# Sevens in a form with plus signs in the weights' sums: two of the four sums by accumulating transfers on GpSimd's queue, two in place

## The chip, the cores and the metric

The kernel runs on one core of a Trainium2 chip. Its metric is the device time of one execution in microseconds. Before the change three runs took 2607.01, 2607.35 and 2611.01 us, so the median is 2607.35 us.

## What is computed

A decoder trunk of two layers on 256 tokens of width 2048, all in float32. Each layer is a token mixer and a SwiGLU feed-forward block, each with a norm ahead of it, a scale and shift from the conditioning vector, and a gate behind it. Layer 0 mixes by retention, layer 1 by a short gated convolution. The change lies in the feed-forward block of layer 1:

```python
def swiglu(h, w_in, w_out):
    a, b = jnp.split(h @ w_in, 2, axis=-1)
    return (jax.nn.silu(a) * b) @ w_out
...
        x = (x + g2 * swiglu(h, ffn_w_in[i], ffn_w_out[i])).astype(x.dtype)
```

Here `h` is 256 x 2048, `w_in` 2048 x 11264 and `w_out` 5632 x 2048.

## The kernel before

All weights are laid out by the host in the order of use, in chunks of 128 partitions x 2048 columns (1 MB). `fetch` (L381) takes one of three buffers named `raw` and has SyncE's queue (SP) load the next chunk into it. TensorE works on float32 as a sum of two rounded parts, so every chunk is split: `prepare` (L387) takes it in pieces; ScalarE rounds a piece to `hi` (L413) and VectorE subtracts that from the piece to get `lo` (L416). There are four buffers each of `hi` and `lo`, so a piece can be rounded as soon as TensorE has finished the piece four places ahead of it. The matmuls take `hi` and `lo` through `take` (L430). TensorE's order is the order of the program; the other engines' order is made by a scheduler that follows priorities, and each engine and queue then works strictly in its own order.

In the feed-forward block of layer 1 the tokens are the output's rows: `token_products` (L1193) computes a block of 256 tokens x 1024 columns, from steps of two 128-row tiles of the weights and two column blocks of 512. A step is one chunk of 1 MB, and there are two kinds:

- A plain step takes the chunk in two pieces of 1024 columns. Each of the four 128 x 512 blocks is multiplied with both halves of the tokens, three matmuls of 512 columns for each product (`triple`, L1182, L1187 to L1189): 24 matmuls.
- A step called seven computes the same 2 x 2 x 2 product of blocks with seven products in place of eight: 21 matmuls. It needs four sums of the activations' blocks (`seven_sums`, L630, made once and used by all column blocks), and four sums of the weights' blocks. Some of the seven products are collected in banks of their own (m1, m5, m6, m7) over all sevens of the block, and added to the output's blocks at the end (L1236 to L1241).

Write B11, B21 for the two row tiles in the first column block, and B12, B22 for those in the second. Before, a seven's chunk holds B11, B12, B22, B21 in that order, and the weights' sums are T1 = B12 - B11, T3 = B22 - B12, T2 = B22 - T1 and T4 = B21 - T2. VectorE makes them in a buffer of its own named `sums` (128 x 4 x 512, one buffer): T1 and T3 in one subtraction 1024 wide (L419), T2 (L423) and T4 (L425) in one each of 512. The seven's pieces are B11 alone (512 wide, one product), B22 and B21, T1 and T3, T2 and T4 (1024 wide, two products each). Since the last two pieces come out of `sums`, the chunk's `raw` buffer is free as soon as T4 is made.

There are 42 sevens: three in each of the ten column blocks of the first matrix that are done this way (30), and four in each of three blocks of the second matrix (12). Between two sevens stand one to three plain steps. The first eight chunks of the block are done in another form (`normed`, L664), which also takes the norm's root on the way: VectorE's L585, GpSimd's power on 128 x 2 numbers (L587) and TensorE's spreading of it (L594).

GpSimd's queue has in this part of the program nothing but that power, and it issues no transfer in the whole kernel.

Of the kernel before, what the change touches and what calls it, by code (L numbers as in the profile page):

```python
# [10 lines left out]
F32 = mybir.dt.float32  # L11
# [3 lines left out]
ALU = mybir.AluOpType  # L15
PSUM = bass.MemoryType.PSUM

P = 128
# [7 lines left out]
DV = 512  # L26
# [5 lines left out]
CHUNK = 2048  # L32
# [22 lines left out]
RAW_BUFS = 3  # L55
PART_BUFS = 4
# [8 lines left out]
class Group:  # L65
# [202 lines left out]
def trunk(ctx: ExitStack, tc: tile.TileContext, x_in, c_in, pos_in, w_mod, cols_in, tab_in, w_all, out):  # L268
    nc = tc.nc
# [8 lines left out]
    def name(s):  # L278
        serial[0] += 1
        return f"{s}_{serial[0]}"  # L280
# [87 lines left out]
    pieces, at_col = [], 0  # L368
    for _, _, g in in_use_order():
        width = sum(w for _, _, w in g.blocks())  # L370
        for o in range(-at_col % HALF, width, HALF):
            i = (at_col + o) % CHUNK
            if not g.seven:
                pieces.append(("plain", i))
            elif i == 0:
                pieces += [("seven", n) for n in range(4)]
        at_col += width
# [3 lines left out]
    def fetch():  # L381
        raw = wpool.tile([P, CHUNK], F32, tag="raw", name=name("raw"), bufs=RAW_BUFS)
        nc.sync.dma_start(raw, w_all[n_fetched[0]])
        n_fetched[0] += 1
        fetched.append(raw)

    def prepare(between=None):  # L387
# [10 lines left out]
        full = raws[0]  # L398
        if kind == "plain":
            raw = full[:, i : i + HALF]  # L400
        else:
            if i == 0:
                blocks[:] = [spool[0].tile([P, 4, DV], F32, tag="sums", name=name("sums"), bufs=1)]
            block = [full[:, n * DV : (n + 1) * DV] for n in range(4)]
            t1, t3, t2, t4 = [blocks[0][:, n, :] for n in range(4)]
# [12 lines left out]
        if kind == "seven" and i == 0:  # L418
            nc.vector.tensor_tensor(  # L419
                blocks[0][:, 0:2, :].rearrange("p a b -> p (a b)"), full[:, DV : 3 * DV], full[:, : 2 * DV],  # L420
                op=ALU.subtract,
            )
            nc.vector.tensor_tensor(t2, block[2], t1, op=ALU.subtract)  # L423
        elif kind == "seven" and i == 1:
            nc.vector.tensor_tensor(t4, block[3], t2, op=ALU.subtract)  # L425

    blocks, spool = [], []
# [203 lines left out]
    def seven_sums(full, tag):  # L631
# [4 lines left out]
        nc.vector.tensor_tensor(s1, a21, a22, op=ALU.add)  # L636
        nc.vector.tensor_tensor(s2, s1, a11, op=ALU.subtract)
        nc.vector.tensor_tensor(s3, a11, a21, op=ALU.subtract)
        nc.vector.tensor_tensor(s4, a12, s2, op=ALU.subtract)
# [554 lines left out]
    def token_products(steps, act, sums_of, then):  # L1194
# [8 lines left out]
        for n, g in enumerate(steps):  # L1203
            first, last = n == 0, n == len(steps) - 1
            if not g.seven:
# [15 lines left out]
                ("m1", a11), (x_banks[1][0], s4), (x_banks[0][0], a12), ("m5", s1), ("m7", s3), ("m6", s2),  # L1221
                (x_banks[0][1], a22),
# [11 lines left out]
            if g is sevens[-1]:  # L1234
                m1, m5, m6, m7 = [flat(m_banks[i]) for i in ("m1", "m5", "m6", "m7")]
                y11, y12, y21, y22 = values = [value(f"y{i}") for i in range(4)]  # L1236
                nc.scalar.copy(y11, m1)
                nc.vector.tensor_tensor(y12, m6, y11, op=ALU.add)
                nc.vector.tensor_tensor(y21, m7, y12, op=ALU.add)
                nc.vector.tensor_tensor(y12, m5, y12, op=ALU.add)  # L1240
                nc.vector.tensor_tensor(y22, m5, y21, op=ALU.add)  # L1241
# [185 lines left out]
```

## Time and profile before

| | |
|---|---|
| median of three runs | 2607.35 us (2607.01 to 2611.01) |
| the profiled execution's own time | 2605.66 us |
| its span in the profile | 2603.9 us |
| TensorE matmul, busy | 2571.1 us, 14341 matmuls |
| VectorE, busy | 2178.4 us |
| ScalarE, busy | 1300.3 us |
| GpSimd, busy | 129.6 us |
| mean rate of the transfers | 264 GB/s |

Times in the profile are counted from the start of the span. PE is TensorE (PEld its weight loads), DVE VectorE, ACT ScalarE, POOL GpSimd, SP SyncE's queue. A group's row gives the line in the kernel, the engine, the operation, what it writes and reads with its shape, how often it occurs, its busy time and mean time, and the idle time of its engine right before it with what ended it. The sevens lie between 1925 and 2513 us of the span.

### The profile page before, as it was taken

What the parts mean: (1) busy time and instruction counts of PE and PEld (TensorE: products, weight loads), DVE (VectorE), ACT (ScalarE), POOL (GpSimd) and SP (SyncE); (2) the same over time, 40 slices, a digit from 0 to 9 for tenths busy, and PEclk for the clock granted to TensorE, in tenths of its full rate; (3) what the DMA queues carried; (4) which work ended last, traced back from release to release, by engine and by line L of the source; (5) the groups of instructions that cost most, each with busy time, mean ns of one, the idle gap of its engine ahead of it and who ended that gap; (6) DMA issues with size and microseconds to landing.
All of it is one profiled execution on the core that took longest, in us unless ns stands there. A gap on an engine that the chain in (4) does not pass through costs nothing.

```text
span 2603.9 us, 36702 instructions
## 1 busy us (share of the span) xinstructions
PE 2571.1 (99%) x14341; PEld 2239.5 (86%) x14341; DVE 2178.4 (84%) x2751; ACT 1300.3 (50%) x1757; POOL 129.6 (5%) x230
## 2 busy tenths in 40 slices
PE   7999999999999999999999999999999999999998
PEld 5998889888889888888888898888898888888887
DVE  7998878787698887777777889888889999999984
ACT  5544543444456444334444454444565554555553
POOL 0000000120000010010000100000000000000000
PEclk9999999999999999999999999999999999999999
DMA  9976668777676887888887868877755555555553
GB/s 399 402 278 239 231 229 323 273 284 279 252 286 243 330 324 292 290 307 304 293 296 285 306 236 317 316 296 279 287 179 209 180 208 201 189 202 198 196 195 129
DMA packets 96945, 687.48 MB, mean 264 GB/s; under 512 B 10753, under 2 KB 12545, under 8 KB 13825
## 3 DMA queue, kind: packets, MB, share of 16 engines
q1 hardware_dynamic: 96194, 684.48, 71.2%
q8 instruction: 112, 1.84, 0.3%
q10 hardware_dynamic: 576, 0.66, 0.1%
q14 instruction: 63, 0.52, 0.1%
HBM read 682.99 MB, written 2.10 MB: 263 GB/s over the span
## 4 chain that ended last, share of the span: by engine, by line
PE 66%; issue 28%; DVE 3%; DMA 2%; ACT 1%; POOL 0%; SPq 0%; POOLq 0%; ACTq 0%; DVEq 0%
PE bank L475 29%; PE bank L478 15%; PE bank L514 4%; PE bank L513 4%; PE bank L515 4%; DMA raw<-w_all 2%; PE bank L499 1%; PE bank L498 1%; PE bank L500 1%; PE bank L688 1%; DVE lo L416 1%; PE bank L689 1%; PE bank L543 1%; PE bank L690 1%; PE bank L542 1%
## 5 line engine op out<-in xcount | busy, mean ns | idle before, releaser
L413 ACT CAST hi<-raw 128x1024 fp32r<-128x1024 f32 (+1 forms) x912 | 932.3, 1031 | 904.2 <-DMA raw<-w_all 268.3
L416 DVE TENSOR_TENSOR lo<-raw,hi 128x1024 fp32r<-128x1024 f32 (+1 forms) x912 | 1081.0, 1196 | 281.2 <-ACT hi L413 278.8
L475 PE MATMUL bank<-h,hi 128*128 128x512 f32 x2016 | 699.8, 391 | 0.0
L478 PE MATMUL bank<-h,lo 128*128 128x256 f32 x2016 | 564.4, 280 | 0.0
L475 PEld LDWEIGHTS bank<-h,hi 128*128 128x128 f32 x2016 | 377.0, 187 | 82.5
L327 DVE SCALAR_TENSOR_TENSOR raw<-raw,cb 128x2048 f32<-128x2048 f32 x160 | 365.8, 2286 | 33.0 <-DMA raw<-w_mod 32.6
L478 PEld LDWEIGHTS bank<-h,lo 128*128 128x128 f32 x2016 | 381.0, 189 | 0.0
L475 PE MATMUL bank<-mid,hi 128*128 128x512 f32 x922 | 321.1, 395 | 0.0
L478 PE MATMUL bank<-mid,lo 128*128 128x256 f32 x922 | 256.1, 278 | 0.3 <-DVE lo L416 0.3
L475 PEld LDWEIGHTS bank<-mid,hi 128*128 128x128 f32 x922 | 172.9, 188 | 40.5
L513 PE MATMUL bank<-hi,h 128*128 128x512 f32 x512 | 201.7, 394 | 0.0
L514 PE MATMUL bank<-lo,h 128*128 128x512 f32 x512 | 200.9, 392 | 0.1
L515 PE MATMUL bank<-hi,h 128*128 128x512 f32 x512 | 200.0, 391 | 0.0
L1187 PE MATMUL bank<-hi,h 128*128 128x512 f32 x490 | 191.5, 391 | 0.0
L1189 PE MATMUL bank<-hi,h 128*128 128x512 f32 x490 | 190.7, 389 | 0.0
L1188 PE MATMUL bank<-lo,h 128*128 128x512 f32 x490 | 190.7, 389 | 0.0
L478 PEld LDWEIGHTS bank<-mid,lo 128*128 128x128 f32 x922 | 173.3, 188 | 0.6 <-DVE lo L416 0.6
L475 PE MATMUL bank<-rm,hi 128*128 128x512 f32 x496 | 173.0, 395 | 0.0
L413 ACT CAST hi<-sums 128x1024 fp32r<-128x1024 f32 x84 | 88.4, 1052 | 143.2 <-PE bank L1189 104.0
L416 DVE TENSOR_TENSOR lo<-sums,hi 128x1024 fp32r<-128x1024 f32 x84 | 102.8, 1223 | 50.4 <-ACT hi L413 50.1
L478 PE MATMUL bank<-rm,lo 128*128 128x256 f32 x496 | 137.7, 278 | 0.0
L515 PEld LDWEIGHTS bank<-hi,h 128*128 128x128 f32 x512 | 96.6, 189 | 20.7
(230 smaller groups left out, 4098.1 us busy)
## 6 DMA issues: line engine op xcount, KB each, us to landing
raw<-w_all SPq DMA_DIRECT2D x456, 1024.0 KB, 4.9
raw<-w_mod SPq DMA_DIRECT2D x192, 1024.0 KB, 5.5
x<-x_in SPq DMA_DIRECT2D x4, 512.0 KB, 5.2
decay<-tab_in SPq DMA_DIRECT2D x8, 128.0 KB, 3.4
out<-x SPq DMA_DIRECT2D x4, 256.0 KB, 3.2
out<-x ACTq DMA_DIRECT2D x3, 128.0 KB, 2.6
out<-x SPq DMA_DIRECT2D x1, 384.0 KB, 2.6
out<-x ACTq DMA_DIRECT2D x1, 256.0 KB, 3.2
```

What stands on the lines that cost most here:

```text
L327: nc.vector.scalar_tensor_tensor(raw, raw, 1.0, cb, op0=ALU.mult, op1=ALU.mult, accum_out=total)
L413: nc.scalar.copy(hi[:, :n], raw)
L416: nc.vector.tensor_tensor(lo[:, :n], raw, hi[:, :n].bitcast(F32), op=ALU.subtract)
L475: nc.tensor.matmul(pt, hi, h, start=fresh and k == g.ks[0], stop=False, skip_group_check=True)
L478: nc.tensor.matmul(pt[:, 1, :], lo, h[:, 0, :], start=False, stop=last and k == g.ks[-1], skip_group_check=True)
L498: nc.tensor.matmul(pt, hi, h[:, 0, :], start=first, stop=False, skip_group_check=True)
L513: nc.tensor.matmul(flat(pt), a[:, 0, :], hi, start=first, stop=False)
L514: nc.tensor.matmul(flat(pt), a[:, 0, :], lo, start=False, stop=False)
L515: nc.tensor.matmul(flat(pt), a[:, 1, :], hi, start=False, stop=last)
L1187: nc.tensor.matmul(flat(pt), a[:, 0, :], hi, start=first, stop=False, skip_group_check=True)
L1188: nc.tensor.matmul(flat(pt), a[:, 0, :], lo, start=False, stop=False, skip_group_check=True)
L1189: nc.tensor.matmul(flat(pt), a[:, 1, :], hi, start=False, stop=last, skip_group_check=True)
```

## The change

The form of the sevens becomes one in which the weights' sums hold plus signs alone: T1 = B11 + B12, T3 = B12 + B22, T2 = B22 + T1, T4 = B21 + T2. The minus signs move to the activations' sums (`seven_sums`) and to the last additions (`y12`, `y22`), one for one.

- The chunk holds the blocks in the order B11, B21, B22, B12.
- `fetch` for a seven's chunk does four transfers in place of one. SP loads the chunk into `raw` as before, and B11 a second time (128 x 512, 256 KB) into a new buffer `sums` (two of these, 512 wide). GpSimd's queue then issues two accumulating transfers of 256 KB each: B22 from the chip's memory is added to B12 in `raw` (giving T3 where B12 stood), and B12 is added to `sums` (giving T1).
- VectorE makes the other two in place in `raw`, after the second piece is split: B22 becomes T2 and then B21 becomes T4 (two additions, 512 wide).
- The pieces become B11 and B21 (1024 wide), B22 and T3 (1024), T1 (512), T4 and T2 (1024), and the seven products are put in the order that takes them so. The last piece is now read from `raw`, which is therefore held until that piece is split.

```diff
-            return [(a, c, DV), (a, d, DV), (b, d, DV), (b, c, DV)]
+            return [(a, c, DV), (b, c, DV), (b, d, DV), (a, d, DV)]
...
     def fetch():
         raw = wpool.tile([P, CHUNK], F32, tag="raw", name=name("raw"), bufs=RAW_BUFS)
-        nc.sync.dma_start(raw, w_all[n_fetched[0]])
+        src = w_all[n_fetched[0]]
+        nc.sync.dma_start(raw, src)
+        if n_fetched[0] in seven_chunks:
+            sums = spool[0].tile([P, DV], F32, tag="sums", name=name("sums"), bufs=SUM_BUFS)
+            nc.sync.dma_start(sums, src[:, :DV])
+            nc.gpsimd.dma_start(raw[:, 3 * DV :], src[:, 2 * DV : 3 * DV], accum_op=ALU.add)
+            nc.gpsimd.dma_start(sums, src[:, 3 * DV :], accum_op=ALU.add)
+            summed_raw.append(sums)
...
-            if i < 2:
-                raw = full[:, 2 * DV * i : 2 * DV * i + (DV, 2 * DV)[i]]
-            else:
-                raw = blocks[0][:, 2 * i - 4 : 2 * i - 2, :].rearrange("p a b -> p (a b)")
+                sums_now[:] = [summed_raw.pop(0)]
+            raw = (full[:, : 2 * DV], full[:, 2 * DV :], sums_now[0], full[:, DV : 3 * DV])[i]
...
-        if kind == "seven" and i == 0:
-            nc.vector.tensor_tensor(
-                blocks[0][:, 0:2, :].rearrange("p a b -> p (a b)"), full[:, DV : 3 * DV], full[:, : 2 * DV],
-                op=ALU.subtract,
-            )
-            nc.vector.tensor_tensor(t2, block[2], t1, op=ALU.subtract)
-        elif kind == "seven" and i == 1:
-            nc.vector.tensor_tensor(t4, block[3], t2, op=ALU.subtract)
+        if kind == "seven" and i == 1:
+            b21, b22 = full[:, DV : 2 * DV], full[:, 2 * DV : 3 * DV]
+            nc.vector.tensor_tensor(b22, b22, sums_now[0], op=ALU.add)
+            nc.vector.tensor_tensor(b21, b21, b22, op=ALU.add)
...
             plan = [
-                ("m1", a11), (x_banks[1][0], s4), (x_banks[0][0], a12), ("m5", s1), ("m7", s3), ("m6", s2),
-                (x_banks[0][1], a22),
+                ("m1", a11), (x_banks[0][0], a12), (x_banks[1][0], s4), ("m7", s3), ("m5", s1),
+                (x_banks[0][1], a22), ("m6", s2),
             ]
```

On VectorE a seven in the middle of the stage stood so before (its chunk is `raw_3410`; `lo` is the second part of a piece, the number behind it only tells pieces apart):

```order
L416 TENSOR_TENSOR lo_3413_18760<-raw_3410_18756,hi_3412_18759 128x512
L419 TENSOR_TENSOR sums_3411_18758<-raw_3410_18756 128x1024
L416 TENSOR_TENSOR lo_3415_18778<-raw_3410_18756,hi_3414_18777 128x1024
L423 TENSOR_TENSOR sums_3411_18758<-raw_3410_18756,sums_3411_18758 128x512
L425 TENSOR_TENSOR sums_3411_18758<-raw_3410_18756,sums_3411_18758 128x512
L416 TENSOR_TENSOR lo_3417_18795<-sums_3411_18758,hi_3416_18794 128x1024
L416 TENSOR_TENSOR lo_3419_18802<-sums_3411_18758,hi_3418_18801 128x1024
```

The same seven on VectorE after the change:

```order
L420 TENSOR_TENSOR lo_3413_18765<-raw_3410_18758,hi_3412_18764 128x1024
L420 TENSOR_TENSOR lo_3415_18781<-raw_3410_18758,hi_3414_18780 128x1024
L424 TENSOR_TENSOR raw_3410_18758<-raw_3410_18758,sums_3411_18760 128x512
L425 TENSOR_TENSOR raw_3410_18758<-raw_3410_18758 128x512
L420 TENSOR_TENSOR lo_3417_18799<-sums_3411_18760,hi_3416_18798 128x512
L420 TENSOR_TENSOR lo_3419_18809<-raw_3410_18758,hi_3418_18808 128x1024
```

The subtraction 1024 wide is gone, the two of 512 are still there, and the last piece is now read from `raw`. In all VectorE has 42 operations fewer.

On SP's queue, at the start of layer 1's feed-forward block, stood before (each row is one chunk's load):

```order
L383 DMA raw_3297_18161<-w_all 128x2048
L383 DMA raw_3310_18250<-w_all 128x2048
L383 DMA raw_3318_18318<-w_all 128x2048
L383 DMA raw_3328_18397<-w_all 128x2048
L383 DMA raw_3365_18538<-w_all 128x2048
```

There stands now:

```order
L386 DMA raw_3297_18161<-w_all 128x2048
L389 DMA sums_3392_18677<-w_all 128x512
L389 DMA sums_3411_18760<-w_all 128x512
L386 DMA raw_3310_18250<-w_all 128x2048
L386 DMA raw_3318_18318<-w_all 128x2048
```

and further down on the same queue, at the first sevens (chunks `raw_3391`, `raw_3410` and `raw_3425`):

```order
L386 DMA raw_3391_18675<-w_all 128x2048
L386 DMA raw_3403_18737<-w_all 128x2048
L386 DMA raw_3410_18758<-w_all 128x2048
L389 DMA sums_3426_18839<-w_all 128x512
L386 DMA raw_3420_18818<-w_all 128x2048
L386 DMA raw_3425_18837<-w_all 128x2048
```

The small loads stand well ahead of the chunks that they belong to, each as early as a `sums` buffer is free. GpSimd's queue had, from the last gate of layer 1 on, the two powers of L587 and the last scaling alone; now it begins so:

```order
L391 DMA sums_3392_18677<-w_all 128x512
L391 DMA sums_3411_18760<-w_all 128x512
L587 TENSOR_TENSOR rs_3287_18076<-rs_3286_18074,half_74 128x2
L390 DMA raw_3391_18675<-w_all 128x512
L390 DMA raw_3410_18758<-w_all 128x512
L391 DMA sums_3426_18839<-w_all 128x512
L390 DMA raw_3425_18837<-w_all 128x512
L391 DMA sums_3459_19007<-w_all 128x512
L391 DMA sums_3483_19114<-w_all 128x512
L390 DMA raw_3458_19005<-w_all 128x512
```

The first two accumulating transfers have come ahead of the norm's power (`rs_3287`), and 84 in all are queued one behind the other.

More of the change, by code (lines that the diff above doesn't have):

```diff
@@ L55 @@
 RAW_BUFS = 3
+SUM_BUFS = 2
 PART_BUFS = 4
@@ L367, in trunk @@
     order = [(g, *b) for _, _, g in in_use_order() for b in g.taken()]
-    pieces, at_col = [], 0
+    pieces, at_col, seven_chunks = [], 0, set()
     for _, _, g in in_use_order():
@@ L402, in prepare @@
             if i == 0:
-                blocks[:] = [spool[0].tile([P, 4, DV], F32, tag="sums", name=name("sums"), bufs=1)]
-            block = [full[:, n * DV : (n + 1) * DV] for n in range(4)]
-            t1, t3, t2, t4 = [blocks[0][:, n, :] for n in range(4)]
-            if i < 2:
-                raw = full[:, 2 * DV * i : 2 * DV * i + (DV, 2 * DV)[i]]
-            else:
-                raw = blocks[0][:, 2 * i - 4 : 2 * i - 2, :].rearrange("p a b -> p (a b)")
+                sums_now[:] = [summed_raw.pop(0)]
+            raw = (full[:, : 2 * DV], full[:, 2 * DV :], sums_now[0], full[:, DV : 3 * DV])[i]
         hi = wpool.tile([P, HALF], F32R, tag="hi", name=name("hi"))
```

11 lines of the change are left out of this document (6 added, 5 removed).

## The prediction

> **What bounds the kernel now.** I read the page's head first, for the shares of the engines, and then only the stretch in which the change lives.
>
> ```profile
> span 2603.9 us, 36702 instructions
> ...
> PE 2571.1 (99%) x14341; PEld 2239.5 (86%) x14341; DVE 2178.4 (84%) x2751; ACT 1300.3 (50%) x1757; POOL 129.6 (5%) x230
> ```
>
> TensorE is busy 99% of the span. That is a mean over stages, so the second view is the table by stretches, cut to the sevens, 1925 to 2513 us:
>
> ```profile
> 1925.00:2513.00 588.00, 587.62 (x2641) 484.89 (x2640) 533.29 (x632) 331.13 (x376) 0.00 (x0) 1.00 0.56 198
> ```
>
> The columns are TensorE, its weight loads, VectorE, ScalarE, GpSimd, the granted clock, the transfers' share and GB/s. TensorE idles 588.00 - 587.62 = 0.38 us in 588 us, at full clock; VectorE has 54.7 us left, the transfers are at 56%. The third view is the waits of the same stretch, longest first:
>
> ```profile
> ACT hi L413 <- PE bank L1189: 205.3, 155, 2.6
> DVE lo L416 <- ACT hi L413: 52.9, 47, 1.6
> ACT hi L413 <- DVE lo L416: 25.8, 26, 1.7
> ```
>
> The splitting waits for TensorE (205.3 us, for a free `hi` buffer), not TensorE for the splitting. No row of this view has ScalarE or VectorE waiting for a load of `raw`. So the stage runs at TensorE's pace, and whatever frees VectorE can bring back at most 0.4 us of it.
>
> **VectorE, less work: worth nothing here.** What goes and what stays:
>
> ```profile
> L419 DVE TENSOR_TENSOR sums<-raw 128x1024 f32<-128x1024 f32 x42 | 51.2, 1219 | 0.0
> ...
> L425 DVE TENSOR_TENSOR sums<-raw,sums 128x512 f32<-128x512 f32 x42 | 28.9, 689 | 0.7
> L423 DVE TENSOR_TENSOR sums<-raw,sums 128x512 f32<-128x512 f32 x42 | 28.8, 686 | 0.1
> ```
>
> The 42 subtractions of 1.219 us go: 51.2 us. The two additions of 512 stay in the count and width of L423 and L425. VectorE falls from 533.3 to about 482 us of 588. All of it was hidden by TensorE's 587.62 us, so its worth is between 0 and 0.4 us; I take 0. The signs in `seven_sums` and in the last additions change no operation's count or shape: 0. TensorE's seven products are put in another order, with the same 21 matmuls and the same weight loads: 0.
>
> **The accumulating transfers: hidden if they land in time.** This is the open term, since no transfer of GpSimd is in the trace. The question is how long one may take, and I work it out on the tightest kind of seven that I found. Its load, the split of its second piece, and TensorE's use of it stand in the timeline:
>
> ```profile
> 2166.61 0.33 SPq L383 DMA_DIRECT2D raw<-w_all  x1
> 2176.32 1.06 ACT L413 CAST hi<-raw 128x1024 fp32r<-128x1024 f32 x1 [0.69 <-PE bank L1189]
> 2182.88 1.23 DVE L416 TENSOR_TENSOR lo<-sums,hi 128x1024 fp32r<-128x1024 f32 x1 [1.05 <-ACT hi L413]
> 2181.56 0.39 PE L1187 MATMUL bank<-hi,mids 128*128 128x512 f32 x1
> 2184.96 0.39 PE L1187 MATMUL bank<-hi,msums 128*128 128x512 f32 x1
> ```
>
> and the time from issue to landing of the stretch's 110 loads of `raw` (the next two rows):
>
> ```profile
> L383 SPq DMA_DIRECT2D raw<-w_all x110: 327/328/328, 1929.1 to 2509.4; - x110
> ...
> DMA to landing us min/median/max: 4.6/4.8/6.2
> ```
>
> The chunk lands at 2166.61 + 4.8 = 2171.4. Its second piece, which is to hold T3, is rounded at 2176.32, when a `hi` buffer comes free: 4.9 us later. Behind that wait there is more. TensorE starts the seven at 2181.56 and its fourth piece, after five products, at 2184.96. From the second piece's rounding to the fourth piece's `lo` lie a rounding (1.06), a subtraction (1.23), two additions (0.69 each), a rounding (1.06) and a subtraction (1.23): 5.96 us. So the rounding may start as late as 2184.96 - 5.96 = 2179.0, 2.7 us after it did. An accumulation may thus take 4.9 + 2.7 = 7.6 us from the chunk's landing, GpSimd's issue included, before TensorE stands. The two other kinds have more room:
>
> ```profile
> 2368.26 0.33 SPq L383 DMA_DIRECT2D raw<-w_all  x1
> 2379.20 1.06 ACT L413 CAST hi<-raw 128x1024 fp32r<-128x1024 f32 x1 [0.97 <-PE bank L1189]
> 2376.40 0.33 SPq L383 DMA_DIRECT2D raw<-w_all  x1
> 2390.64 1.06 ACT L413 CAST hi<-raw 128x1024 fp32r<-128x1024 f32 x1 [0.76 <-PE bank L1189]
> ```
>
> By the same sum they have 2379.20 - 2373.06 + 2.7 = 8.8 us and 2390.64 - 2381.20 + 2.7 = 12.1 us. I count the three kinds as a third of the 42 each.
>
> Now the price of one accumulation. The nearest rows are transfers of other sizes, at the page's end and in a stretch (1860 to 1876 us) where the loads overlapped:
>
> ```profile
> x<-x_in SPq DMA_DIRECT2D x4, 512.0 KB, 5.2
> ...
> out<-x SPq DMA_DIRECT2D x4, 256.0 KB, 3.2
> ...
> raw<-w_all SPq DMA_DIRECT2D x5, 1024.0 KB, 6.8
> ```
>
> From below: a plain transfer of 256 KB took 3.2 us. From above: 6.8 us, as a whole chunk among other loads, and 0.7 us for GpSimd to issue (its smallest operation, L587 below), 7.5 us. An accumulation has to read what it adds to as well, 512 KB, so it is nearer to the rows of 256 and 512 KB than to the last; I take 4.5 us, which is under 4.9: nothing shifts. Even 7.5 us is under 7.6. The Trainium skill (DMA: Bandwidth & Descriptors, Anatomy of one DMA) gives a transfer of GpSimd about 2.0 us and its bytes at 436 GB/s, an estimate of 2.6 us for 256 KB by that page; with it the sum would be the same 0, and this trace's 3.2 us speaks for a little more.
>
> The other accumulation, into `sums`, starts from a load that SP issues as soon as the `sums` buffer of two sevens before is free, some 20 us ahead of its use: hidden, and the VectorE addition that needs it finds it done. GpSimd's queue holds nothing else there (0.00 us in the stretch's row), so nobody waits behind it. The bytes are 42 x 3 x 0.26 = 33 MB more in 588 us, 56 GB/s on 198, or 94 with the read of the destination. The page's slices show what the transfers can carry, 402 in the second:
>
> ```profile
> GB/s 399 402 278 239 231 229 323 273 284 279 252 286 243 330 324 292 290 307 304 293 296 285 306 236 317 316 296 279 287 179 209 180 208 201 189 202 198 196 195 129
> ```
>
> Hidden too.
>
> **The raw buffer, held longer.** A seven's buffer came free after L425; now it is held until the fourth piece's `lo`. The load three chunks later starts then. At the tightest place:
>
> ```profile
> L425 DVE TENSOR_TENSOR sums<-raw,sums x1: 684/684/684, 2361.3 to 2361.3; 128x512 f32<-128x512 f32 x1
> 2362.07 0.33 SPq L383 DMA_DIRECT2D raw<-w_all  x1
> 2364.64 1.23 DVE L416 TENSOR_TENSOR lo<-sums,hi 128x1024 fp32r<-128x1024 f32 x1 [0.89 <-ACT hi L413]
> 2370.99 1.05 ACT L413 CAST hi<-raw 128x1024 fp32r<-128x1024 f32 x1 [1.67 <-PE bank L1189]
> 2378.95 0.39 PE L1187 MATMUL bank<-hi,h 128*128 128x512 f32 x1
> ```
>
> The issue moves from 2362.07 (just behind L425) to 2364.64 + 1.23 = 2365.9, the landing to 2370.7, still ahead of the rounding at 2370.99. If the load takes the 6.8 us of overlapped ones, rounding is 1.7 us late; it and its subtraction take 2.3 us and TensorE comes at 2378.95, 5.7 us after 2373.3: no stall. Term: 0, up to a load of 10 us.
>
> **The start of the block.** Two small loads and two accumulations now stand ahead of work that matters: on SP ahead of chunk loads, on GpSimd ahead of the norm's power. They wait for the memory of the convolution's tiles, at the latest for its last matmul:
>
> ```profile
> 1877.55 0.28 PE L500 MATMUL bank<-mid,lo 128*128 128x256 f32 x1
> 1884.17 0.71 POOL L587 TENSOR_TENSOR rs<-rs,half 128x2 f32<-128x2 f32 x1 [17.75 <-DVE rs L585]
> 1888.15 0.61 PE L594 MATMUL bank<-tab,rs 128*128 128x128 f32 x4
> ```
>
> From 1877.8 a load of 3.2 us and two issues of 0.7 us bring GpSimd to 1882.5, before 1884.17. The power's result is used at 1888.15, so 3.3 us more are spare. Term: 0; if each issue held GpSimd for 4 us, it would cost 2 us once.
>
> **The sum.** 0 to -0.4 for VectorE, 0 for the rest: span 2603.9, with the 1.8 us around it 2605.7 in an execution like the profiled one, whose own time is 1.7 us under the median. I give the median unchanged, 2607.3.
>
> **The rivals.** First, the accumulations land late. From 7.6 us on TensorE stands at each seven of the tight kind and from 8.8 us at the next. At 9 us that is 14 x 1.4 + 14 x 0.2 = 22 us, 2629 us; at 10 us 14 x 2.4 + 14 x 1.2 = 50 us, 2657 us. Slower. For it: the operation is not in the trace, and an accumulation that ran at a third of a load's rate would be there. Against it: the room is more than twice the 3.2 us of a transfer of this size, and right after the tight chunk's landing no other load runs, since the next one is held back.
>
> Second, VectorE shuts GpSimd out while it writes its transfers' orders. VectorE is busy 533.29 of 588 us, in runs; its pauses are 52.9 us in 47 pieces (the waits' second row), 1.1 us each. With the 51.2 us that it is relieved of there are about twice as many, one every 588 / 94 = 6.2 us. An accumulation that has to find one takes 4.5 us and 0 to 6.2 more. For the tight kind the mean excess over 7.6 us is 3.1 x 3.1 / 2 / 6.2 = 0.8 us, for the next 1.9 x 1.9 / 2 / 6.2 = 0.3: 14 x 1.1 = 15 us, 2622 us; it decides from a wait of 3.1 us on. Slower as well. The Trainium skill (SBUF — State Buffer, Who interferes with whom) says that VectorE in a two-port mode locks GpSimd out of a shared port, and that two-input operations like these have no such mode and take only its read side, which writing orders does not need; by that the rival falls away. The stretch has no GpSimd work beside VectorE's, so no row here shows it, and I keep the rival at a small chance.
>
> Third, VectorE's relief is worth something after all. It would need stalls of TensorE that the waits don't show: 0.38 us in the row of the stretch. The most that I can make of it is a few tenths here and some us if the transfers' new rhythm moved the first stall elsewhere: 2602 us. Faster; it decides only if TensorE idle outside 0.4 us is found.
>
> **How the numbers follow.** A measurement of this kernel can tell about 0.2%, 5.2 us, from no change. Forecast (hidden): 0.72. Late accumulations 0.16, GpSimd shut out 0.07, together slower 0.23. Relief worth over 5.2 us: 0.05. The likeliest time is 2607.3. The range goes from 2604 (the forecast less 0.4 and the scatter of a median) to 2630, which takes in both slower rivals up to accumulations of 9 us, about half of their chance; left out are 0.05 below and some 0.11 above.
>
> **What would show it.** Right: in the sevens' stretch TensorE's idle time stays under 1 us, VectorE's busy time falls by about 51 us, ScalarE's waits for TensorE (205.3 us) grow or stay, a new row of ScalarE waiting for an accumulation is absent or short, and GpSimd's transfers land within 5 us. Wrong: a row of TensorE waiting for `hi` or `lo` at L1187 to L1189 with `raw<-w_all` of GpSimd's queue behind it, landings over 7.6 us, a root (L587) later than 1888, or TensorE's count or mean time of L1187 to L1189 changed.

## The result and the profile after

| | before | after |
|---|---|---|
| median of the runs beside each other | 2607.18 us (2606.63 to 2611.01, 4 runs) | 2704.47 us (2701.19 to 2710.39, 4 runs) |
| profiled execution: span | 2603.9 us | 2699.4 us |

The ratio is 1.0375, with an interval of 1.036 to 1.039: the change is 97 us slower. The prediction said no difference, and its range ended at 2630.

The head of the page after, and its rows of the transfers in the sevens (KB each, and the median from issue to landing):

```profile
span 2699.4 us, 37037 instructions
...
PE 2601.3 (96%) x14341; PEld 2252.0 (83%) x14341; DVE 2140.9 (79%) x2709; ACT 1298.3 (48%) x1757; POOL 203.8 (8%) x314
...
sums<-w_all SPq DMA_DIRECT2D x42, 256.0 KB, 3.2
...
sums<-w_all POOLq DMA_DIRECT2D x42, 256.0 KB, 7.0
...
raw<-w_all POOLq DMA_DIRECT2D x42, 256.0 KB, 5.0
```

TensorE does the same 14341 matmuls and VectorE has the 42 operations fewer, as planned. The accumulations took 5.0 us (into `raw`, T3) and 7.0 us (into `sums`, T1) at the median, where the prediction took 4.5. The same stretch as before, 1925 to 2513 us, in the table by stretches:

```profile
1925.00:2513.00 588.00, 531.20 (x2267) 426.76 (x2266) 423.14 (x510) 282.12 (x322) 62.52 (x72) 0.96 0.72 215
```

TensorE now idles 588.00 - 531.20 = 56.8 us where it idled 0.4, and the granted clock is 0.96 in place of 1.00. In 588 us it got 2267 of the 2641 matmuls done. The 374 that are missing are 374 x 0.2225 = 83 us at the pace of before (588 us by 2641). So 56.8 us of this are idle time, and the remaining 26 a slower pace. (The rest of the 97 us falls behind 2513 us, where the longer stage still runs.) The waits of the stretch tell what ended last:

```profile
...
ACT hi L417 <- DMA raw<-w_all: 119.9, 31, 8.3
ACT hi L417 <- PE bank L1189: 113.2, 101, 2.7
...
PE bank L1187 <- DVE mids L1281: 32.9, 8, 4.1
...
PE bank L1188 <- DVE lo L420: 12.8, 20, 0.8
```

The first of these rows is new: ScalarE, which before waited for TensorE and VectorE but for no transfer, stands 31 times for a load or an accumulation into `raw`, up to 8.3 us; 93.8 us of it, in 16 waits, are for the accumulations. The last two are TensorE's own waits. The loss is not spread evenly. More than half of the idle time sits in the first sevens of column blocks, eight times 4.5 to 5.9 us, seven of them in the first matrix. Over all 42 sevens it divides cleanly: in 25 the accumulation into `raw` landed at most 6.2 us after its chunk, and TensorE did not stand; in the other 17 it landed 7.3 to 9.8 us after, and TensorE idled 1.5 to 5.8 us in each. One of the long ones, in the chain of work that ended last (start, length, what):

```profile
1966.13 7.56 DMA raw<-w_all
...
1974.37 9.07 DMA raw<-w_all
...
1983.54 1.05 ACT hi L417
...
1984.62 1.24 DVE lo L420
...
1987.17 0.61 DVE raw L425
...
1987.88 1.05 ACT hi L417
...
1988.96 1.01 DVE lo L420
...
1990.10 1.29 DVE mids L1281 x2
...
1991.44 0.80 PE bank L1187
1992.23 0.43 PE bank L1188
```

The chunk's load takes 7.56 us, the accumulation of T3 starts 0.7 us after its landing and takes 9.07. Only then can ScalarE round the second piece. In ScalarE's and VectorE's fixed orders stand behind it T2, T4 and their split, and behind those the rounding of the previous block's turned output (`mids`, L1280 and L1281), whose bank TensorE needs next. TensorE's timeline of the same place:

```profile
1984.64 0.49 PE L1187 MATMUL bank<-hi,rows 128*128 128x512 f32 x1 [0.97 <-ACT hi L417]
1985.90 0.50 PE L1188 MATMUL bank<-lo,rows 128*128 128x512 f32 x1 [0.76 <-DVE lo L420]
...
1991.44 0.80 PE L1187 MATMUL bank<-hi,rows 128*128 128x512 f32 x1 [4.11 <-DVE mids L1281]
```

It stands 0.97 + 0.76 us for the split of T3's piece and then 4.11 us for the bank. What the stall costs beyond itself is in the table by stretches around its end (the clock is the number ahead of the last two):

```profile
1984.64:1990.44 5.80, 1.92 (x6) 1.04 (x6) 4.58 (x6) 3.02 (x5) 0.00 (x0) 0.72 0.42 90
1990.44:1991.44 1.00, 0.00 (x1) 0.00 (x1) 1.00 (x3) 1.00 (x3) 0.61 (x1) 0.50 0.55 74
1991.44:1997.35 5.91, 5.91 (x14) 4.71 (x15) 4.19 (x5) 3.00 (x3) 0.26 (x1) 0.50 0.93 298
1997.35:2003.00 5.65, 5.65 (x27) 4.64 (x26) 3.88 (x8) 2.13 (x3) 0.87 (x1) 0.99 0.35 133
```

For 5.9 us after the stall TensorE is busy but at a granted clock of 0.50, with 14 matmuls where the next 5.65 us hold 27. The clock is at 0.50 before the stall ends: by the 0.72 of the first row it fell at about 1987.2 us, where the long stall begins. There are eight such spells in the stretch, 51.2 us in all. TensorE is busy for 38.8 us of them, and half of that, 19 us, is most of the 26 us of slower pace; what makes up the rest was not traced.

### The profile page after: what moved, and what is told of

Its sections match the earlier page's. It is cut to its first block, busy times and chain, and to the rows that moved or that the text cites. A ratio compares the mean times of both kernels' runs of the same rounds, so it can differ in the third digit from the quotient of the medians.

```text
span 2699.4 us, 37037 instructions
## 1 busy us (share of the span) xinstructions
PE 2601.3 (96%) x14341; PEld 2252.0 (83%) x14341; DVE 2140.9 (79%) x2709; ACT 1298.3 (48%) x1757; POOL 203.8 (8%) x314
## 3 DMA queue, kind: packets, MB, share of 16 engines
q0 software_dynamic: 12096, 22.03, 5.3%
## 4 chain that ended last, share of the span: by engine, by line
PE 79%; DMA 10%; DVE 7%; ACT 2%; issue 2%; POOL 0%; SPq 0%; ACTq 0%; POOLq 0%; DVEq 0%
PE bank L475 30%; PE bank L478 16%; DMA raw<-w_all 9%; PE bank L513 4%; PE bank L514 4%; PE bank L515 4%; DVE lo L420 4%; PE bank L1187 3%; PE bank L1188 3%; PE bank L1189 3%; ACT hi L417 2%; PE bank L500 1%; PE bank L499 1%; PE bank L498 1%; PE bank L688 1%
## 5 line engine op out<-in xcount | busy, mean ns | idle before, releaser
L420 DVE TENSOR_TENSOR lo<-raw,hi 128x1024 fp32r<-128x1024 f32 x954 | 1155.8, 1222 | 454.0 <-ACT hi L417 443.0
L417 ACT CAST hi<-raw 128x1024 fp32r<-128x1024 f32 x954 | 989.4, 1050 | 1080.8 <-DMA raw<-w_all 439.2
L515 PEld LDWEIGHTS bank<-hi,h 128*128 128x128 f32 x512 | 96.5, 189 | 20.7
L1188 PEld LDWEIGHTS bank<-lo,h 128*128 128x128 f32 x490 | 94.2, 192 | 22.2 <-DVE lo L420 2.6
L513 PEld LDWEIGHTS bank<-hi,h 128*128 128x128 f32 x512 | 96.8, 189 | 17.7
```

The costliest lines, as they stand in the source:

```text
L417: nc.scalar.copy(hi[:, :n], raw)
L420: nc.vector.tensor_tensor(lo[:, :n], raw, hi[:, :n].bitcast(F32), op=ALU.subtract)
L513: nc.tensor.matmul(flat(pt), a[:, 0, :], hi, start=first, stop=False)
L515: nc.tensor.matmul(flat(pt), a[:, 1, :], hi, start=False, stop=last)
L1188: nc.tensor.matmul(flat(pt), a[:, 0, :], lo, start=False, stop=False, skip_group_check=True)
```

## The experiments

In the expectations below theory 1 puts the loss on the accumulating transfers, theory 2 on the `raw` buffer that is held to the last piece, so that loads come late and together.

**VectorE makes the sums.** Form, order and hold of the change, without any extra transfer:

```diff
-            nc.sync.dma_start(sums, src[:, :DV])
-            nc.gpsimd.dma_start(raw[:, 3 * DV :], src[:, 2 * DV : 3 * DV], accum_op=ALU.add)
-            nc.gpsimd.dma_start(sums, src[:, 3 * DV :], accum_op=ALU.add)
...
+                nc.vector.tensor_tensor(sums_now[0], full[:, :DV], full[:, 3 * DV :], op=ALU.add)
+                nc.vector.tensor_tensor(full[:, 3 * DV :], full[:, 3 * DV :], full[:, 2 * DV : 3 * DV], op=ALU.add)
```

> The changed kernel with neither small load nor accumulating transfer: VectorE makes T1 in the sums buffer and T3 in place in raw (two additions of 512 more per seven), everything else as after the change, the raw buffer held to the last piece included. Theory 1 (the accumulations land late beside the chunk loads): no row of TensorE waiting behind a transfer is left in the sevens' stretch, its idle there is under 2 us in place of 59.7, time 2605 to 2612 us. Theory 2 (the longer hold of raw bunches the chunk loads, and that alone is enough): TensorE still idles over 20 us there, time over 2640 us. VectorE's busy time in the stretch is back near 535 us with both.

Measured: 2604.79 us against 2605.82 for the kernel before in the same job, ratio 0.9993 (0.9984 to 1.0003), just under theory 1's range. The stretch:

```profile
1925.00:2513.00 588.00, 587.52 (x2644) 486.17 (x2643) 539.36 (x672) 330.83 (x376) 0.00 (x0) 1.00 0.54 198
```

TensorE idles 0.5 us. So the new form, its order of products and the hold cost nothing here. The loss needs the transfers. Theory 2 alone falls. One more thing differs in this kernel: on ScalarE the scheduler has put the rounding of the turned output (here L1279) ahead of the fourth piece's, where the change has it behind (1987.88 and 1988.83 us):

```profile
2019.27 1.07 ACT L1279 CAST mids<-bank 128x512 fp32r<-128x512 f32 x2 [2.20 <-PE bank L1258]
2020.23 1.06 ACT L416 CAST hi<-raw 128x1024 fp32r<-128x1024 f32 x1
...
1987.88 1.04 ACT L417 CAST hi<-raw 128x1024 fp32r<-128x1024 f32 x1 [2.78 <-DVE raw L425]
1988.83 1.07 ACT L1280 CAST mids<-bank 128x512 fp32r<-128x512 f32 x2
```

The first two rows are of this kernel, the last two of the change. That this order alone does not make the loss is shown further down: the kernels with both sums ahead and with T3 last have the change's order and the hold, and lose next to nothing.

**Raw freed early.** All transfers as in the change, but T2 and T4 go to a buffer of their own, so that `raw` is free after T4 as before the change:

```diff
+                sums_now.append(spool[0].tile([P, 2, DV], F32, tag="t42", name=name("t42"), bufs=1))
...
-            nc.vector.tensor_tensor(b22, b22, sums_now[0], op=ALU.add)
-            nc.vector.tensor_tensor(b21, b21, b22, op=ALU.add)
+            t4, t2 = [sums_now[1][:, n, :] for n in range(2)]
+            nc.vector.tensor_tensor(t2, b22, sums_now[0], op=ALU.add)
+            nc.vector.tensor_tensor(t4, b21, t2, op=ALU.add)
```

> The changed kernel, but T2 and T4 go to a tile of their own in place of B22 and B21, so that raw is free after T4 as it was before the change; transfers as after. Theory 1 (late accumulations): they still share the engines with two chunk loads, land 6 to 9 us after their issue at the first seven of a column block; TensorE still idles over 30 us, time 2660 to 2705 us. Theory 2 (the hold): the loads are spread as before, accumulations land within 5 us, time 2607 to 2620 us.

Measured: 2624.85 us (2620.02 to 2643.24), ratio 1.0087 (1.0057 to 1.0117). Its stretch, and the landing of its accumulations into `raw`:

```profile
1925.00:2513.00 588.00, 575.21 (x2564) 471.74 (x2563) 475.07 (x574) 321.21 (x368) 71.20 (x82) 0.99 0.82 245
```

```profile
DMA to landing us min/median/max: 4.0/6.2/8.8
```

This fits neither theory. Over the stretch the accumulations are no faster (6.2 us at the median against 4.9 in this stretch of the change), though in the first sevens of the blocks they are (6.9 us against 8.4), and some four fifths of the loss are gone. The hold costs nothing without the transfers, and the transfers cost 19 us without the hold (15 to 31 by the interval), and 97 us with it: the two can't be told as separate terms of a sum.

**Plain transfers on GpSimd's queue.** The two accumulations become copies of the same bytes to the same places. This kernel leaves out the two additions, T1 and T3 hold other numbers:

```diff
-            nc.gpsimd.dma_start(raw[:, 3 * DV :], src[:, 2 * DV : 3 * DV], accum_op=ALU.add)
-            nc.gpsimd.dma_start(sums, src[:, 3 * DV :], accum_op=ALU.add)
+            nc.gpsimd.dma_start(raw[:, 3 * DV :], src[:, 2 * DV : 3 * DV])
+            nc.gpsimd.dma_start(sums, src[:, 3 * DV :])
```

> The changed kernel with plain transfers in place of the two accumulating ones, of the same size, on GpSimd's queue, with the same waits; it leaves out the two additions, so the sevens' weights are not the reference's. If accumulating is what costs (reading and writing the destination): landings of 3 to 4 us from issue in place of 5.0 and 7.0, time under 2640 us. If it is the queue and the sharing with the chunk loads: landings and time like the changed kernel's, over 2680 us.

Measured: 2638.2 us in one run. The queue's row here (packets, MB, share of 16 engines' span):

```profile
q0 software_dynamic: 6720, 22.03, 3.3%
```

and that of the change:

```profile
q0 software_dynamic: 12096, 22.03, 5.3%
```

An accumulation of 256 KB is 12096 / 84 = 144 packets, a copy 80, and its packets take 5.3 / 3.3 = 1.6 times as long on the transfer engines. The copies into `raw` landed after 4.1 us at the median, the accumulations after 5.0. Without the accumulating part 32 us of loss are left, so in this company it is worth about 65.

**The turned output earlier.** The rounding of the turned output (L1280, L1281), which stood in the chain above, is scheduled half a plain step sooner (8 of its 16 units):

```diff
-        return [(8, lambda: product_of(0)), (8, lambda: product_of(1)), (16, turned)]
+        return [(8, lambda: product_of(0)), (8, lambda: product_of(1)), (8, turned)]
```

> The changed kernel with the turning of a finished block (L1259, and its evacuation L1280 and L1281 on ScalarE and VectorE) put 8 units earlier in TensorE's program, ahead of the first seven of the next block. Theory 1a (half of the loss is TensorE waiting for a bank whose evacuation stands behind the late rounding in ScalarE's and VectorE's own order: 39.0 us in the waits' row): that row is gone, and with it part of the slow clock behind the stalls; time 2640 to 2665 us. If that wait only runs beside the late accumulation: TensorE waits as long for hi or lo, time over 2690 us.

Measured: 2710.08 us in one run, no gain. TensorE's waits in the same stretch:

```profile
PE bank L1188 <- DVE lo L420: 23.4, 38, 0.8
PE bank L1187 <- ACT hi L417: 9.3, 12, 2.9
PE bank L1187 <- ACT full L1284: 7.7, 7, 1.1
```

The wait for L1281 (32.9 us) is gone, and waits for `lo`, `hi` and L1284 stand in its place. The turned output was only the last of several things behind the late rounding, and not a cause of its own here. That theory fell.

**One sum by transfer, the other by VectorE.** Two kernels, to see which accumulation costs. From here on theory A is that an accumulation costs where it starts only after the chunk has landed and the next piece waits for it (T3, in `raw`). Theory B is that the bytes and packets cost, whichever sum they make. First T1 alone by transfer:

```diff
-            nc.gpsimd.dma_start(raw[:, 3 * DV :], src[:, 2 * DV : 3 * DV], accum_op=ALU.add)
...
+                nc.vector.tensor_tensor(full[:, 3 * DV :], full[:, 3 * DV :], full[:, 2 * DV : 3 * DV], op=ALU.add)
```

> Only T1 comes from a transfer (the small load on SP and one accumulating transfer into the buffer of its own); T3 is made by VectorE in place, 0.69 us as the others. The raw buffer is held as in the changed kernel. Theory A: what costs is the accumulation into raw, since it can start only once the chunk has landed and the second piece waits for it; T1's is 20 us ahead of its use. Then this kernel is near the one with VectorE's sums: 2603 to 2615 us, TensorE's idle time in the sevens under 4 us. Theory B: what costs is what the accumulations take from the transfers (their bytes and packets), whichever sum they make. Then half of the loss stays: 2640 to 2665 us.

Measured: 2629.28 us in one run, 24 us over the kernel before. Then T3 alone:

```diff
-            nc.sync.dma_start(sums, src[:, :DV])
+            nc.sync.dma_start(sums, src[:, 3 * DV :])
...
-            nc.gpsimd.dma_start(sums, src[:, 3 * DV :], accum_op=ALU.add)
...
+                nc.vector.tensor_tensor(sums_now[0], sums_now[0], full[:, :DV], op=ALU.add)
```

> Only T3 comes from an accumulating transfer, into raw; for T1 SP loads a block into the buffer of its own by a plain transfer and VectorE adds to it. The raw buffer is held as in the changed kernel. Theory A (the accumulation into raw is on the path from the load to TensorE): most of the loss stays, 2670 to 2705 us, with the waits of ScalarE for GpSimd's transfers at the first seven of each block. Theory B (bytes and packets): half of it, 2640 to 2665 us.

Measured: 2623.2 us in one run, 18 us over. Both theories missed: neither half carries the loss, and 24 + 18 is less than half of 97. What T1's transfer does although it is early is in the waits of the first of these kernels:

```profile
DVE raw L412 <- DMA raw<-w_all: 41.7, 23, 4.2
```

VectorE's own addition for T3 (L412) waits here for the chunk's landing, and all that stands behind it in VectorE's order waits too. With VectorE making both sums the same kind of wait was 7.8 us in the stretch, since there the loads of the sevens' stretch landed after 4.8 us at the median. Beside T1's two transfers they take 6.8 us. So T1 is harmless to its own reader, but it lengthens the load that T3 has to wait for.

**Both sums ahead of time.** T1 and T3 both in a buffer of their own, begun before the chunk's load lands, with the same bytes accumulated and 256 KB a seven more loaded:

```diff
+            sums = spool[0].tile([P, 2 * DV], F32, tag="sums", name=name("sums"), bufs=SUM_BUFS)
+            nc.sync.dma_start(sums, src[:, : 2 * DV])
+            nc.gpsimd.dma_start(sums, src[:, DV : 3 * DV], accum_op=ALU.add)
...
+            raw = (full[:, :DV], full[:, 2 * DV :], sums_now[0], full[:, 2 * DV :])[i]
...
-                ("m1", a11), (x_banks[0][0], a12), (x_banks[1][0], s4), ("m7", s3), ("m5", s1),
-                (x_banks[0][1], a22), ("m6", s2),
+                ("m1", a11), (x_banks[1][0], s4), (x_banks[0][0], a12), ("m5", s1), ("m7", s3), ("m6", s2),
+                (x_banks[0][1], a22),
```

With this the pieces and products are back in the order of the kernel before, so T3 is taken with T1 in the third piece and no longer in the second. The kernel moves two things at once.

> Both T1 and T3 are made ahead of time in a buffer of their own of 1024 columns: SP loads B11 and B12 into it, one accumulating transfer of 512 KB on GpSimd's queue adds B12 and B22; VectorE makes T2 and T4 in place in raw as in the changed kernel, and raw is held to the last piece. The same bytes are accumulated as in the changed kernel, and 256 KB a seven more are loaded. Theory A (only an accumulation that starts after the chunk's landing costs): 2603 to 2615 us, under 4 us of TensorE idle in the sevens. Theory B (the accumulations' bytes and packets slow the chunks' loads): 2650 to 2710 us, with the chunk loads of the first sevens at 7 us or more.

Measured: 2606.36 us against 2605.51, ratio 1.0007 (0.9996 to 1.0018). The stretch, the landing of its chunk loads, and ScalarE's wait for them:

```profile
1925.00:2513.00 588.00, 586.57 (x2636) 484.08 (x2635) 494.19 (x589) 330.63 (x376) 34.76 (x40) 1.00 0.84 269
```

```profile
DMA to landing us min/median/max: 4.7/7.5/11.6
```

```profile
ACT hi L416 <- DMA raw<-w_all: 39.3, 19, 6.0
```

The transfers are busier than in the change (0.84 against 0.72) and the chunk loads slower (7.5 us at the median against 6.9), but nothing is lost. Theory B falls with this. Slow loads are harmless here, where nothing stands between the landing and the split of the second piece. Whether the early start of T3 or its later place does it, this kernel can't tell; the next one tests the place alone.

**T3 taken last.** The sharpest test: every transfer of the change stays, and T3's place among the pieces moves from the second to the last, so that there are five pieces in place of four.

```diff
-            raw = (full[:, : 2 * DV], full[:, 2 * DV :], sums_now[0], full[:, DV : 3 * DV])[i]
+            raw = (full[:, : 2 * DV], full[:, 2 * DV : 3 * DV], sums_now[0], full[:, DV : 3 * DV], full[:, 3 * DV :])[i]
...
-                ("m1", a11), (x_banks[0][0], a12), (x_banks[1][0], s4), ("m7", s3), ("m5", s1),
-                (x_banks[0][1], a22), ("m6", s2),
+                ("m1", a11), (x_banks[0][0], a12), (x_banks[1][0], s4), ("m5", s1), (x_banks[0][1], a22),
+                ("m6", s2), ("m7", s3),
```

> The changed kernel with one thing moved: T3, the sum that an accumulating transfer makes in raw, is taken last instead of in the second piece. The pieces are B11 and B21, B22 alone, T1, T4 and T2, T3 alone; the products follow them. All transfers stay as they are. Theory A (a due time: T3 is ready too late for the second piece): in the first sevens of the blocks T3's rounded part was ready 15.7 us after TensorE's start two steps before, and due at 13.1; as the last product it is due at 15.75. So most of the stall should go: 2610 to 2645 us, the rest being what stands behind T3's rounding on ScalarE. Theory B (the transfers' traffic slows the stage as a whole, whatever waits for what): 2680 to 2710 us.

> The control for the kernel with T3 last: the same five pieces and products, but both sums made by VectorE and no transfer for them. It tells what the five pieces alone cost (two more narrow splits a seven, 42 x 0.15 us of VectorE, and less work ahead in the hi and lo buffers). If nothing: 2602 to 2610 us. If the shorter lead costs: 2615 to 2640 us, and the kernel with T3 last is to be read against this one.

Measured, one run each: 2608.32 us with the transfers, and 2610.65 us for the control in which VectorE makes both sums, beside 2606.34 for the kernel before. All but 2 of the 97 us are gone, more than theory A had said (2610 at the least), and the control is just over the 2610 of its better case. Single runs of the kernel before lie between 2602 and 2611, so neither 2 us nor 4 us can be told from nothing. The stretch with T3 last, the landing of its accumulations into `raw`, and TensorE's longest wait there:

```profile
1925.00:2513.00 588.00, 585.34 (x2619) 480.46 (x2619) 491.88 (x627) 334.41 (x417) 70.62 (x81) 1.00 0.82 249
```

```profile
DMA to landing us min/median/max: 4.0/6.7/9.8
```

```profile
PE bank L1188 <- DVE lo L420: 2.7, 7, 0.5
```

The accumulations are as slow as ever, 6.7 us at the median and 9.8 at most, and nobody misses them. Theory A holds, in a wider form: work between the chunk's landing and a piece that TensorE needs early, be it an accumulation or a waiting addition of VectorE, costs once load and work together end after the piece's due time. Times in the first sevens of the blocks, each column a median of its own over the 13, in us from TensorE's start of the step two ahead (due is when TensorE takes the piece if nothing has delayed it; its `lo` is needed 0.2 us later):

| | load issued | landed | accumulation into raw landed | piece with T3: rounding begins | its `lo` done | due |
|---|---|---|---|---|---|---|
| after | -4.9 | 3.1 | 12.1 | 12.2 | 14.5 | 13.1 |
| raw freed early | -4.9 | 0.5 | 7.9 | 8.0 | 10.3 | 13.1 |
| T3 alone by transfer | -4.9 | 0.0 | 5.5 | 5.7 | 8.5 | 13.1 |
| T3 taken last | -4.4 | 1.6 | 7.2 | 13.4 | 15.2 | 15.9 |
| VectorE's sums | -4.9 | 0.0 | - | 6.9 | 9.2 | 13.1 |

The 15.7 in the expectation for T3 last was 1.2 too high: 14.5 is the end of the subtraction, and the split was 1.4 us late and not 2.6. The table shows that the hold does not move the issue of this load (-4.9 in each of the kernels that take T3 in the second piece). What it moves is the load one chunk ahead: that was issued at -10.3 with raw freed early and at -7.6 in the change, so that more of it runs beside this one. With the hold and both accumulations the landing moves by 3.1 us and the accumulation stretches from 4.3 us after GpSimd's issue (T3 alone) to 8.4. With T3 last the same load lands 1.5 us earlier than in the change. That this comes from ScalarE no longer standing is a guess, and how much of its lateness the change makes itself was not separated.

The table also shows where theory A ends. With raw freed early and with T3 alone by transfer the piece with T3 is split 2.8 and 4.6 us before its due time, and these kernels still lose 19 and 18 us. TensorE's longest wait in both is for the bank of the turned output, whose rounding stands behind the fourth piece's:

```profile
PE bank L1191 <- DVE mids L1285: 6.5, 4, 3.5
...
PE bank L1187 <- DVE mids L1281: 8.2, 8, 1.7
```

The first row is of the kernel with raw freed early, the second of that with T3 alone. So the fourth piece, T4 and T2, has a due time too, and with it what is queued behind it. In the control with VectorE's sums the turned output is rounded ahead of that piece. How much of the 18, 19 and 24 us this order explains was not tested.

**Attempts at a faster kernel.** The narrower `sums` buffer leaves the memory for a fourth seven in each column block of the first matrix, 30 matmuls fewer. First with VectorE's sums:

```diff
-IN_SEVENS = {0: (), 1: (2, 4, 6)}
+IN_SEVENS = {0: (), 1: (2, 4, 5, 6)}
...
-SUM_BUFS = 2
+SUM_BUFS = 1
```

> A try at a faster kernel, without any transfer for the sums. VectorE makes all four sums (T1 in a buffer of 512 columns, the others in place), which frees 6 KB a partition against the kernel before, enough for a fourth seven in each of the ten column blocks of the first matrix (row pairs 2, 4, 5 and 6 in place of 2, 4 and 6). If the stage stays at TensorE's pace it saves 10 x 3 matmuls of 0.2225 us (588 us by 2641 matmuls), 6.7 us: 2596 to 2601 us, ratio 0.9975. VectorE gets 10 x 2.75 us more, about 566 of 581 us. Rival: three sevens in a row with the raw buffer held to the last piece take a chunk every 4.7 us, and a load of 4.8 us that starts late makes TensorE wait: 2605 to 2625 us.

Measured: 2645.59 us, ratio 1.0154 (1.0139 to 1.0169).

```profile
1925.00:2513.00 588.00, 562.28 (x2450) 451.79 (x2449) 551.12 (x698) 325.70 (x377) 0.00 (x0) 0.99 0.50 183
```

VectorE has 37 us left over the stretch, but a seven gives it four additions and 4.35 us of splits, 7.1 us for TensorE's 4.7, and by this sum three in a row put it 7.2 us behind. The one `sums` buffer in place of two is another difference, and was not tested by itself. I then tried the form with T3 last, which has two additions fewer:

```diff
-IN_SEVENS = {0: (), 1: (2, 4, 6)}
+IN_SEVENS = {0: (), 1: (2, 4, 5, 6)}
```

> A try at a faster kernel: the form with T3 last and both sums by transfers, and a fourth seven in each column block of the first matrix (row pairs 2, 4, 5 and 6, as in the kernel with four sevens by VectorE; the narrower sums buffers leave the memory for it). VectorE has for a seven two additions and five splits, 2 x 0.69 + 2 x 1.22 + 3 x 0.69 = 5.9 us, against 7.1 us with all sums made by VectorE and TensorE's 4.7 us. If the loss of that kernel was VectorE's pace in three sevens in a row (7.2 us behind in each block, now 3.6), and the accumulations land in time, the stage is TensorE's and saves 6.7 us: 2597 to 2604 us. Rival: three chunks in a row with two accumulations each fall behind the due time of T3: 2615 to 2670 us.

```diff
-IN_SEVENS = {0: (), 1: (2, 4, 6)}
+IN_SEVENS = {0: (), 1: (2, 3, 5, 6)}
```

> The same with the four sevens as two pairs (row pairs 2, 3, 5 and 6), so that no more than two stand in a row. VectorE is 2.4 us behind in a pair. If the length of the row is what counts, this one is the better: 2596 to 2603 us. Rival: the accumulations of a pair collide as those of three do, 2610 to 2650 us.

Measured: 2692.78 us, ratio 1.0333 (1.0319 to 1.0347), and as two pairs 2662.82 us, 1.0216 (1.0202 to 1.0231). Both are slower than even their rivals' ranges, and not for the rivals' reason: for the accumulations of T3 ScalarE waits only 2.3 and 4.2 us in the stretch. In the first kernel it waits for T4, and also for T1's accumulation, which no longer comes early:

```profile
ACT hi L417 <- DVE raw L425: 36.2, 18, 2.3
ACT hi L417 <- DMA sums<-w_all: 29.2, 9, 5.0
```

The relief of VectorE came together with the transfers, so these runs don't show whether VectorE's pace is what limits four sevens. The chain through T2 and T4 in fixed order would do it as well, and that stays open. No version beat the kernel before.

## Why the prediction was wrong

- **What bounds the kernel: right.** With VectorE's sums the stretch is TensorE's for 587.52 of 588 us, and VectorE's relief is worth nothing (both sums ahead: VectorE 494 us in place of 533, the same time).
- **The accumulation's price: the first failed step.** I took 4.5 us, "nearer to the rows of 256 and 512 KB". Alone that is about right: 4.2 us at the median where T3 alone is accumulated, and 4.4 in the change's 29 sevens that are not the first of a block. In the first sevens it was 8.4. My upper end of 7.5, "as a whole chunk among other loads", assumed that an accumulation meets loads as a plain transfer does. In the first sevens of the kernel with plain transfers a copy took 5.0 us.
- **"Right after the tight chunk's landing no other load runs": false, and the main reason.** It was false in the trace before already: the tight chunk was issued at 2166.61 and landed 4.8 us later, at 2171.4, and the next load followed at once, in the row below. In the long example after the change two loads run beside the accumulation (issued at 1969.59 and 1974.38 us, the accumulation at 1974.37). And the load itself, which I left at 4.8 us as before, took 7.5 at the median of the first sevens.

```profile
2171.86 0.33 SPq L383 DMA_DIRECT2D raw<-w_all  x1
```

- **The sum that failed.** For a first seven I had a load of 4.8 us and an accumulation of 4.5, 9.3 us from the load's issue, against a room of 13.6. By the table's medians the load's landing came 8.0 us after its issue and the accumulation's another 9.0, together 17.0: both terms were too small, by 3.2 and 4.5 us, and it is 3.4 late.
- **T1's transfers and the extra bytes, "hidden too": right for their reader, wrong for their neighbour.** T1 was there in time, but its transfers, alone, lengthen the stretch's chunk loads from 4.8 to 6.8 us, and T3 waits for such a load.
- **The hold, "0, up to a load of 10 us": right alone, wrong in company.** The prediction held each term by itself against a room that all of them share. Alone they cost 0 (hold), 24 (T1) and 18 us (T3), all together 97.
- **The room: about right; which kind is tight: wrong.** The prediction let an accumulation take 7.6 to 8.8 us from the chunk's landing, and TensorE stood in just those sevens in which it took 7.3 us or more. But the seven on which I worked out the tight kind belongs to the second matrix, and TensorE idled 2.5 us in it, half of what it did in most first sevens of the first matrix. The "third of the 42 each" was a guess: by the loads' landings in the trace before, only six of the 42 have no more than the 4.9 us from landing to rounding that made the kind tight. What uses the room up differs from seven to seven with the loads beside it.
- **The rivals.** The first, late accumulations, is what happened, at a chance of 0.16. Its price was too small because it counted only the lateness: 13 first sevens x 3.4 us = 44 us. It lacked what stands behind the late rounding in fixed orders (4.1 us for a bank in the example, 1.7 for the split itself) and the half clock at the long stalls (19 us in the stretch). The second, VectorE shutting GpSimd out, was not seen: GpSimd's issue of the accumulation took 0.9 us and came 0.7 us after the landing. The third found nothing.
- **The start of the block: right.** The power began at 1884.69 us against 1884.17.

## What to carry to other kernels

Work on data that has just landed has a due time: count back from the piece's use, and take the load and what follows it at the pace that they have beside each other, not each at its pace alone. Small costs that are each hidden by the same room are to be added up before they are held against it, and a transfer that is early for its own reader can still be late for its neighbour's. If a late sum can't be made sooner, use it later: here the order of seven products was worth some 95 us.

## What the runs showed of the hardware

- **An accumulating transfer.** 256 KB took 4.2 us at the median where T3 alone was accumulated, and in the change 7.0 at the median and up to 10.8 us (T1's, in the stretch). The Trainium skill (DMA: Bandwidth & Descriptors, Anatomy of one DMA) gives a fit of 2.0 us and the bytes at 436 GB/s for GpSimd's transfers, by which I estimate 2.6 us. Plain copies on that queue took 3.3 us at the least and accumulations 3.9, so the measurement is over this estimate in every run here.
- **The clock at a stall.** In the example the granted clock was 0.50 from about 1987.2 us, the beginning of the 4.1 us stall, to 5.9 us after its end; TensorE had stood for 0.97 and 0.76 us just before. The eight spells at 0.50 in the stretch lasted 3.4, 6.8 or 10.2 us, with 2.9 to 6.2 us of work until full speed. The Trainium skill (TensorE: Matmul & The Clock Gate, Part 1: The HAM clock gate) has half rate after an idle window of about 3.4 us and full rate after a busy one of the same length. The trace agrees on the half and on spells of one, two or three times 3.4 us; the way back took between a little less than one such length and nearly two, and in the example the clock fell without 3.4 us of unbroken idle time.
